# Beside work held to its tick on VectorE and ScalarE, GLA outputs one block later, value blocks in turning banks, matvec at 1.0 in the key stage

## The chip, the cores and the metric

The kernel runs on one core of a Trainium2 chip. Its engines work side by side, each through its own queue: TensorE (PE) multiplies matrices into the eight banks of PSUM, VectorE (DVE) and ScalarE (ACT) work element by element, GpSimd (POOL) and SyncE (SP) mostly issue transfers. The metric is the time of one execution in device microseconds, as the median of the runs shown. A second number, the span, is taken by the hardware profiler in one execution, from the first to the last instruction.

## The reference

One layer of a flow-matching backbone over 256 latent tokens with 256 context tokens, width 2048, all in f32. Cut to what matters here:

```python
qa, ka, va, qb, kb, vb, rb, lrf, lrb, gate_a, gate_b = jnp.split(h @ w_in, offs, axis=-1)
# A: 16 query and 4 key heads of 128, QK-norm, rotary, window of 128, context keys, sink
o_attn = windowed_attention(q, k, v, k_ctx, v_ctx, sink)
# B: gated linear attention, 4 heads (dk 256, dv 512), both directions, started from the context
of, _ = gla_chunked(q, k, v, gf, sf)
ob, _ = gla_chunked(flip(q), flip(k), flip(v), flip(gb), sb)
y_att = o_attn @ w_attn_o
y_gla = (rms_norm(o_gla, gla_norm).reshape(B, T, GLA_V_WIDTH) * jax.nn.silu(rb)) @ w_gla_o
x = x + mod_x[2] * ((jax.nn.sigmoid(gate_a) * y_att + jax.nn.sigmoid(gate_b) * y_gla) @ w_out)
x = x + mod_x[5] * conv_ffn(modulate(x, g_ffn, mod_x[3], mod_x[4]), w_up, conv_w, conv_b, w_down)
```

`mod_x` are six vectors of 2048, `silu(c) @ w_mod + b_mod`. Four of them (numbers 2 to 5) are made beside the main work: they are the matvec of this document.

## The kernel before

**Products.** Every f32 factor is split into two fp32r halves, hi and lo, and a product is three matmuls: hi·hi, lo·hi and hi·lo. Weights are streamed: `wload` (L180) brings two 128-row tiles by 512 columns, 512 KB, into one of seven buffers `raw`; `wsplit` (L186) makes `whi` on ScalarE and `wlo` on VectorE, with high priority for the scheduler. `proj_nat` (L195) multiplies one 512-column block of a weight matrix, step by step over two row tiles: first the hi products of all token blocks, then the lo products. Its accumulators are one PSUM bank for each token block (four for latent and context, two for the latent tokens alone), held over the whole block and emptied by `evac` at its end.

**PSUM.** Eight banks: four take turns under the tag `acc`; three, `side`, and one, `main`, serve the beside work (L61).

**Order.** `tick()` (L152) is called at the start of each step of a block. It sets `pin` to the last product issued, lowers the counters of the deferred pieces in `later` and calls those that are due (`defer(n, fn)` runs at the tick after n more), advances the generator in `beside` by its rate, and lets `pace()` take `bg_rate` steps of `bg_steps`. So the program says where beside work belongs. In the opening stage `in_order` ties each engine to that order. After it the framework's scheduler decides, when the kernel is built: it puts into each engine's queue what it expects to be ready, in the order of the program where there is a choice. What `mm_b` and `turn_b` (L82, L85) issue in a tick gets an edge (`after`, L75) that keeps it behind `pin`; the edge is of the class NoSync, so it fixes the order of building and is no semaphore. VectorE's and ScalarE's beside work has no such edge. Loads on SP have no order after the opening (L698).

**Stages around the change**, with what runs beside them:

| products | steps | beside |
|---|---|---|
| second half of the GLA keys, `kb_block` (L922) | 8 | GLA head 0 |
| GLA values of heads 1, 2, 3, `v_block` (L887) | 3 x 8 | GLA heads 1, 2, 3 |
| attention keys (L989), attention values (L990) | 2 x 8 | key norm and rotary, transposes `ptk` |
| four query blocks and the first gate block (L1064 to L1072) | 5 x 8 | attention of one key head each |
| GLA gate `rb` (L1101), merge (L1111 to L1135) | 4 x 8, 120 | transposes |
| `w_out` (L1177), ConvFFN | | matvec of `w_up`'s shift, then the last of `mod_x` |

The matvec (L316) runs through the first five rows: 96 steps for three vectors, each step one 512 KB `raw` load and two VectorE instructions (`macc`, L337 or L339); the load of the next step is issued with the step. Its rate is 0.3 a tick beside the GLA blocks, 1.6 in the key and value stage, 0.0 in the attention and 0.52 from the GLA gate on. After 8 steps a column block is transposed, summed (L345), and three ticks later `out` (L347) turns it by a small matmul into the bank `pcl`.

`gla_A` (L751) makes the two attention factors of a head in 13 pieces at 1.65 a tick: gates in two pieces, eight levels of which each takes exponentials (L812 to L820), products with q and k (L814, L821), running sums (L823 to L826) and, one piece later, matmuls into `pa`; then the scans and `kf`, `kg` (L844 to L853), and two pieces later the cross products with `kf` and `kg` (L860). `gla_o` (L866) multiplies both factors with the head's values, 24 matmuls into `po` for its two token blocks, and is called as soon as the value block is emptied, ahead of the next block. The values are split into hi and lo straight from their banks (`split`, L65).

The large SBUF tiles (`M`, L55) share 16 buffers.

Of the kernel before, what the change touches and what calls it, by code (L numbers as in the profile page):

```python
# [8 lines left out]
F32 = mybir.dt.float32  # L9
# [7 lines left out]
P = 128  # L17
# [8 lines left out]
QA, KA, VA, QB, KB, VB, RB = 0, 2048, 2560, 3072, 4096, 5120, 7168  # L26
# [4 lines left out]
MODB = [(t, 1) for t in range(4)] + [(t, 2) for t in range(4, 16, 2)]  # L31
DFF = 5632
SCALE = HD ** -0.5


def layer_kernel(ctx, tc, A, out):
    nc = tc.nc
    V, S, G, PE = nc.vector, nc.scalar, nc.gpsimd, nc.tensor
# [9 lines left out]
    acc = pool(name="acc", bufs=4, space=PSUM)  # L48
    ps = pool(name="ps", bufs=1, space=PSUM)

    w_in = A["w_in"][0]
# [6 lines left out]
    def W2(tag, name, shape, dt=F32):  # L58
        return f2.tile(shape, dt, name=name, tag=tag, bufs=F2_BUFS[tag])

    def bank(name, shape=(P, 512), side=False):  # L61

        return ps.tile(list(shape), F32, name=name, tag="side" if side else "main", bufs=3 if side else 1)

    def split(hi, lo, src):  # L65
        S.activation(hi, src, AF.Copy)  # L66
        V.tensor_tensor(lo, src, hi.bitcast(F32), op=ALU.subtract)  # L67
# [3 lines left out]
    def mm(*a, **k):  # L71

        last[0] = PE.matmul(*a, **k).ins  # L73

    def after(i):  # L75

        if pin[0] is not None:
            tc.add_manual_dep(i.ins, pin[0].name, mybir.DependencyInfo(
                mybir.DependencyClass.NoSync, mybir.DependencyReason.DATA), reason="place among the products")
        return i  # L80

    def mm_b(*a, **k):  # L82
        return after(PE.matmul(*a, **k))  # L83
# [54 lines left out]
    bg_rate = [0.0, 0.0]  # L138
# [5 lines left out]
    def defer(n, fn):  # L144

        later.append([n, fn])
# [5 lines left out]
    def tick():  # L152

        pin[0] = last[0]
        count[0] += 1
        for e in later:
            e[0] -= 1
        due = [e for e in later if e[0] < 0]
        later[:] = [e for e in later if e[0] >= 0]
        for e in due:  # L160
            e[1]()
        if beside:
            beside[2] += beside[1]
            while beside[2] >= 1.0:
                beside[2] -= 1.0
                next(beside[0], None)
        pace()
        pin[0] = None
# [26 lines left out]
    def proj_nat(w, r0, c0, kts, lhs, evac, get=wsplit, spare=0, banks=None):  # L195

        go = banks is None
        if go:
            banks = [bank("acx", side=True) if i < spare else acc.tile([P, 512], F32, name="acc", tag="acc")
                     for i in range(len(lhs))]  # L200
        for k0 in kts[::2]:
            tick()
            nk = min(2, kts[-1] + 1 - k0)
            hi, lo = get(w[r0 + k0 * P:r0 + (k0 + nk) * P, c0:c0 + 512])
            for i, l in enumerate(lhs):
                for k in range(nk):
                    kt = k0 + k
                    ahi, alo = l(kt)
                    mm(banks[i], ahi, hi[:, k, :], start=(go and kt == kts[0]), stop=False)
                    mm(banks[i], alo, hi[:, k, :], start=False, stop=False)  # L210
            if opening[0]:
                pace()
            for i, l in enumerate(lhs):
                for k in range(nk):
                    kt = k0 + k
                    mm(banks[i], l(kt)[0], lo[:, k, :], start=False, stop=(evac is not None and kt == kts[-1]))
        if evac is None:
            return banks
        for i in range(len(lhs)):
            evac(i, banks[i])  # L220
# [51 lines left out]
    ALL = list(range(KT))  # L272


    def mod_both(b):
# [37 lines left out]
        n_ = 16 // nk  # L313
        return [lambda i=i: get(i) for i in range(n_)], [lambda i=i: step(i) for i in range(n_)] + [fold]

    def matvec(parts, put=lambda fn: defer(3, fn)):  # L316


        seq = [(part, j, k0) for part in parts for j in range(part[4]) for k0 in range(0, KT, 2)]
        raws, a = {}, []  # L320

        def get(i):
            if i < len(seq) and i not in raws:
                (w, c0, _, _, _, _), j, k0 = seq[i]
                raws[i] = wload(w[k0 * P:k0 * P + 256, c0 + j * 512:c0 + (j + 1) * 512])

        def step(i):
            (_, _, vec, dst, _, b0), j, k0 = seq[i]
            get(i)
            get(i + 1)  # L330
            if k0 == 0:
                a[:] = [W2("mod", "macc", [P, 512])]
            raw = raws[i]
            for k in range(2):
                kt = k0 + k
                if kt == 0:
                    V.tensor_scalar(a[0], raw[:, 0, :], vec[:, 0:1], None, op0=ALU.mult)  # L337
                else:
                    V.scalar_tensor_tensor(a[0], raw[:, k, :], vec[:, kt:kt + 1], a[0],  # L339
                                           op0=ALU.mult, op1=ALU.add)  # L340
            if k0 == KT - 2:
                tr = W2("mod", "mtr", [P, 16, 32])
                V.transpose(tr.rearrange("p a c -> p (a c)"), a[0])
                rs = sm.tile([P, 16], F32, name="mrs", tag="mrs", bufs=2)
                V.tensor_reduce(rs, tr, op=ALU.add, axis=AX.X)  # L345

                def out():  # L347
                    pc = bank("pcl", (32, 16))
                    mm_b(pc, sel[:, 0:32], rs, start=True, stop=True)
                    pv = pc.rearrange("p (a b) -> p b a", b=4)  # L350
                    d = dst[:, 4 * j:4 * j + 4]
                    for b4 in range(4):
                        V.tensor_copy(d[32 * b4:32 * b4 + 32, :], pv[:, b4, :])
                    if b0 is not None:
                        V.tensor_tensor(d, d, bmod[:, b0 + j * 4:b0 + j * 4 + 4], op=ALU.add)

                put(out)

        return [lambda i=i: step(i) for i in range(len(seq))]
# [98 lines left out]
    h_xc = h_x + [h_tok(1, 0), h_tok(1, 1)]  # L458
# [61 lines left out]
    kbt = M("kb0", [P, 4, 512])  # L520
# [121 lines left out]
    for gi, (t0, n) in enumerate(groups):  # L642
# [28 lines left out]
        for b in run:  # L671
            keep = more and (b == "V" if gi % 2 == 0 else b[0] == "Q")
            banks = held.pop(b, None)
# [192 lines left out]
    def gla_o(h, a, vh, vl):  # L866
        ats, atc = a
        if h % 2 == 0:
            og.append(M(f"og{h}", [P, 2, 2, 512]))
        for t in range(2):  # L870
            po = bank("po", side=True)
            n = 0
            for s in range(4):
                if s < 2:
                    i = 0 if s == t else 1
                    ah, al = ats[i][:, 0, s, :], ats[i][:, 1, s, :]
                else:
                    ah = atc[0][:, s - 2, t * P:(t + 1) * P]
                    al = atc[1][:, s - 2, t * P:(t + 1) * P]
                for x_, y_ in ((ah, vh), (ah, vl), (al, vh)):  # L880
                    mm_b(po, x_, y_[:, s, :], start=(n == 0), stop=(n == 11))
                    n += 1
            S.activation(og[h // 2][:, h % 2, t, :], po, AF.Copy)
            junk = W2("fb", "junk", [P, 512])
            S.activation(junk, po, AF.Square, accum_out=ssg[:, h, t:t + 1])

    def v_block(c0, name):  # L887
        vh, vl = M(name + "h", [P, 4, 512], F32R), M(name + "l", [P, 4, 512], F32R)
        proj_nat(w_in, 0, c0, ALL, h_xc, lambda i, b: split(vh[:, i, :], vl[:, i, :], b))
        return vh, vl  # L890


# [20 lines left out]
    def with_gla(h, kb, block):  # L913
        res = []
        beside[:] = [gla_A(h, kb, qbt, res), 1.65, 0.0]
        v = block()
        for _ in beside[0]:
            pass
        beside.clear()
        return res, v  # L920
# [6 lines left out]
    a, kb1 = with_gla(0, kbt, kb_block)  # L927
    v = M("v0h", [P, 4, 512], F32R), M("v0l", [P, 4, 512], F32R)
    for i in range(4):
        split(v[0][:, i, :], v[1][:, i, :], vb0[:, i, :])  # L930
    gla_o(0, a, *v)
    for h in (1, 2, 3):
        a, v = with_gla(h, kb1 if h > 1 else kbt, lambda h=h: v_block(VB + h * 512, f"v{h}"))
        gla_o(h, a, *v)


    att = M("att", [P, 2048])
# [47 lines left out]

        defer(2 + i, turn)

    bg_rate[0] = 1.6
    proj_nat(w_in, 0, KA, ALL, h_xc, ka_evac)  # L989
    vah, val = v_block(VA, "va")  # L990

    oh, ol = [], []

# [17 lines left out]
    def attend(g, qT):  # L1011
# [3 lines left out]
        for t in range(2):  # L1015
# [14 lines left out]
            sk = sink[:, 4 * g:4 * g + 4]  # L1030
            V.scalar_tensor_tensor(mx, mx, SCALE, sk, op0=ALU.mult, op1=ALU.max)
            V.tensor_tensor(es, sk, mx, op=ALU.subtract)
            V.tensor_scalar(mx, mx, -1.0, None, op0=ALU.mult)
            S.activation(es, es, AF.Exp)
            for h in range(4):
                S.activation(sc[h], sc[h], AF.Exp, scale=SCALE, bias=mx[:, h:h + 1],  # L1036
                             accum_out=ds_[:, h:h + 1])
# [73 lines left out]
    for j in range(4):  # L1111
# [6 lines left out]
        def at_evac(t, b, a1=a1, j=j):  # L1118
            if j == 0:
# [5 lines left out]
                 lambda t, b, a2=a2: sig.append(S.activation(a2[t], b, AF.Sigmoid)))  # L1125
# [218 lines left out]
```

## Time and profile before

| | us |
|---|---|
| median of 3 runs | 2018.4 (2017.47 to 2019.22) |
| the profiled execution | 2015.55 |
| its span | 2013.3 |
| VectorE busy in it | 1447.0 |
| ScalarE busy in it | 970.6 |

A line of the view of waits names the instruction that waited and, after the arrow, what it waited for last; then the total time in us, how often, and the longest. A line of the timeline gives start and length in us, engine, line, operation, what is written and read, how many instructions are merged (x), and in brackets the idle time of the engine before them. A tile's name stands without its number. [...]

### The profile page before, as it was taken

The numbers are of one execution on the slowest core, as the hardware profiler recorded it, in microseconds if no ns is written. First come the engines' busy times: TensorE is split into PE (matmuls) and PEld (weight loads), VectorE is DVE, ScalarE is ACT, GpSimd is POOL, SyncE is SP. The second block draws the span as 40 slices with busy tenths as digits, with TensorE's granted clock in tenths as the row PEclk, the third lists the DMA queues.
The fourth block names the chain that finished last, engine by engine and source line by source line (L and its number), as shares of the span: only waits on it lengthen the run. The fifth ranks groups of instructions, "written<-read, shape, count | busy, mean of one in ns | idle before, by whom it ended". The sixth has DMA issues, their size and how long they took to land.

```text
span 2013.3 us, 27564 instructions
## 1 busy us (share of the span) xinstructions
PE 1985.8 (99%) x10452; PEld 1649.7 (82%) x10452; DVE 1447.0 (72%) x2246; ACT 970.6 (48%) x1415; POOL 37.2 (2%) x56
## 2 busy tenths in 40 slices
PE   9999999999999999999999999999999999999998
PEld 7778888887777777887778888888888888888887
DVE  5656767887758888877776476899897455667754
ACT  5223565552345656444344445665555434555532
POOL 0001000001000000000000000000000000000000
PEclk9999999999999999999999999999999999999999
DMA  9876222346543456788887586588885655555563
GB/s 390 330 274 218 92 83 86 102 125 205 171 156 116 129 187 203 254 278 270 272 272 239 189 313 209 179 267 270 265 273 199 211 197 189 188 188 188 189 215 110
DMA packets 200437, 417.41 MB, mean 207 GB/s; under 512 B 13040, under 2 KB 13456, under 8 KB 195696
## 3 DMA queue, kind: packets, MB, share of 16 engines
q1 hardware_dynamic: 198816, 411.48, 61.3%
q0 software_dynamic: 1056, 4.08, 0.6%
q8 instruction: 82, 1.34, 0.3%
q14 instruction: 51, 0.42, 0.1%
q10 hardware_dynamic: 432, 0.09, 0.0%
HBM read 413.48 MB, written 2.11 MB: 206 GB/s over the span
## 4 chain that ended last, share of the span: by engine, by line
PE 58%; DMA 5%; DVE 3%; issue 1%; ACT 0%; DVEq 0%; ACTq 0%
PE acc L73 43%; PE accs L73 12%; DMA raw<-in_w_mod 5%; DVE macc L339 2%; DVE wlo L67 1%; PE poa L83 1%; PE pS L83 1%; PE ptp L86 1%; PE pto L86 0%; ACT whi L66 0%; PE ptx L86 0%; DVE s L1041 0%; ACT s L1036 0%; DVE macc L337 0%; PE ptq L86 0%
## 5 line engine op out<-in xcount | busy, mean ns | idle before, releaser
L66 ACT ACTIVATE whi<-raw 128x1024 fp32r<-128x1024 f32 x536 | 567.5, 1059 | 701.3 <-PE acc L73 493.7
L67 DVE TENSOR_TENSOR wlo<-raw,whi 128x1024 fp32r<-128x1024 f32 x536 | 653.7, 1223 | 294.9 <-ACT whi L66 269.1
L339 DVE SCALAR_TENSOR_TENSOR macc<-raw,ccol,macc 128x512 f32<-128x512 f32 x240 | 181.0, 754 | 104.5 <-DMA raw<-in_w_mod 101.1
L73 PE MATMUL acc<-h,whi 128*128 128x512 f32 x672 | 183.8, 395 | 0.0
L73 PE MATMUL accs<-h,whi 128*128 128x512 f32 x672 | 180.3, 390 | 0.0
L73 PEld LDWEIGHTS accs<-h,whi 128*128 128x128 f32 x672 | 126.2, 188 | 28.2
L73 PE MATMUL acc<-whi,ah 128*128 128x512 f32 x352 | 137.1, 389 | 0.0
L73 PE MATMUL acc<-whi,al 128*128 128x512 f32 x352 | 137.1, 389 | 0.0
L73 PE MATMUL acc<-whi,h00hi 128*128 128x512 f32 x336 | 134.1, 399 | 0.5 <-DVE val L67 0.5
L73 PE MATMUL acc<-whi,h01hi 128*128 128x512 f32 x336 | 133.6, 398 | 0.0
L73 PE MATMUL acc<-whi,h00lo 128*128 128x512 f32 x336 | 131.9, 393 | 0.0
L73 PE MATMUL acc<-whi,h01lo 128*128 128x512 f32 x336 | 131.7, 392 | 0.0
L73 PEld LDWEIGHTS acc<-h,whi 128*128 128x128 f32 x672 | 115.6, 190 | 15.1
L73 PEld LDWEIGHTS acc<-h,wlo 128*128 128x128 f32 x672 | 102.7, 189 | 13.1
L73 PE MATMUL accs<-h,wlo 128*128 128x256 f32 x672 | 108.0, 283 | 0.0
L73 PE MATMUL acc<-h,wlo 128*128 128x256 f32 x672 | 106.8, 282 | 0.0
L73 PE MATMUL acc<-wlo,ah 128*128 128x512 f32 x352 | 94.1, 389 | 0.0
L73 PE MATMUL acc<-wlo,h01hi 128*128 128x512 f32 x336 | 93.0, 395 | 0.8 <-DVE wlo L67 0.7
L73 PE MATMUL acc<-wlo,h00hi 128*128 128x512 f32 x336 | 93.5, 393 | 0.1
L73 PEld LDWEIGHTS accs<-h,wlo 128*128 128x128 f32 x672 | 92.7, 192 | 0.0
L73 PEld LDWEIGHTS acc<-wlo,ah 128*128 128x128 f32 x352 | 66.1, 188 | 13.7
L73 PEld LDWEIGHTS acc<-whi,ah 128*128 128x128 f32 x352 | 66.1, 188 | 13.7
(406 smaller groups left out, 3668.0 us busy)
## 6 DMA issues: line engine op xcount, KB each, us to landing
raw<-in_w_in SPq DMA_DIRECT2D x204, 512.0 KB, 4.3
raw<-in_w_up SPq DMA_DIRECT2D x184, 512.0 KB, 3.5
raw<-in_w_mod SPq DMA_DIRECT2D x128, 512.0 KB, 4.2
raw<-in_w_down SPq DMA_DIRECT2D x88, 512.0 KB, 3.6
mraw<-in_k_wm SPq DMA_DIRECT2D x32, 1024.0 KB, 8.7
raw<-in_w_attn_o SPq DMA_DIRECT2D x32, 512.0 KB, 5.1
raw<-in_w_gla_o SPq DMA_DIRECT2D x32, 512.0 KB, 4.7
raw<-in_w_out SPq DMA_DIRECT2D x32, 512.0 KB, 4.7
```

The costliest lines, as they stand in the source:

```text
L66: S.activation(hi, src, AF.Copy)
L67: V.tensor_tensor(lo, src, hi.bitcast(F32), op=ALU.subtract)
L73: last[0] = PE.matmul(*a, **k).ins
L83: return after(PE.matmul(*a, **k))
L86: return after(PE.transpose(*a))
L339: V.scalar_tensor_tensor(a[0], raw[:, k, :], vec[:, kt:kt + 1], a[0], op0=ALU.mult, op1=ALU.add)
```

## The change

Four edits.

- `V` and `S` become wrappers that pass each instruction they issue through `after`. What VectorE and ScalarE get inside a tick is so kept behind the last product before that tick; outside ticks nothing changes, since `pin` is empty there.
- `gla_o` of each head is deferred by one tick count: it runs at the second tick of the next block instead of ahead of it.
- The value blocks of heads 1 and 3 take the bank `main` for their first accumulator (name `acm`), that of head 2 takes four `acc` banks, and the attention value block takes two `side` banks and two `acc` banks. Since `main` is then held by a block, the matvec's column sums `pcl` go to `side` until the key stage, and to `main` from there on.
- The matvec's rate in the key and value stage is 1.0 instead of 1.6.

```diff
+class Placed:
+    def __init__(self, engine, place):
+        self.engine, self.place = engine, place
+
+    def __getattr__(self, name):
+        f = getattr(self.engine, name)
+
+        def call(*a, **k):
+            return self.place(f(*a, **k))
+
+        return call
...
+    V = Placed(V, after)
+    S = Placed(S, after)
...
-            banks = [bank("acx", side=True) if i < spare else acc.tile([P, 512], F32, name="acc", tag="acc")
-                     for i in range(len(lhs))]
+            banks = [bank("acm") if spare < 0 and i == 0 else bank("acx", side=True) if i < spare else
+                     acc.tile([P, 512], F32, name="acc", tag="acc") for i in range(len(lhs))]
...
+    pcl_side = [True]
...
-                    pc = bank("pcl", (32, 16))
+                    pc = bank("pcl", (32, 16), side=pcl_side[0])
...
-    def v_block(c0, name):
+    def v_block(c0, name, spare=0):
...
-        proj_nat(w_in, 0, c0, ALL, h_xc, lambda i, b: split(vh[:, i, :], vl[:, i, :], b))
+        proj_nat(w_in, 0, c0, ALL, h_xc, lambda i, b: split(vh[:, i, :], vl[:, i, :], b), spare=spare)
...
-    gla_o(0, a, *v)
+    defer(1, lambda a=a, v=v: gla_o(0, a, *v))
     for h in (1, 2, 3):
-        a, v = with_gla(h, kb1 if h > 1 else kbt, lambda h=h: v_block(VB + h * 512, f"v{h}"))
-        gla_o(h, a, *v)
+        a, v = with_gla(h, kb1 if h > 1 else kbt, lambda h=h: v_block(VB + h * 512, f"v{h}", -(h % 2)))
+        defer(1, lambda h=h, a=a, v=v: gla_o(h, a, *v))
...
-    bg_rate[0] = 1.6
+    pcl_side[0] = False
+    bg_rate[0] = 1.0
     proj_nat(w_in, 0, KA, ALL, h_xc, ka_evac)
-    vah, val = v_block(VA, "va")
+    vah, val = v_block(VA, "va", 2)
```

## The prediction, made before the result was known

> **What bounds the kernel now.** I read the page's busy shares first, then its chain.
>
> ```profile
> PE 1985.8 (99%) x10452; PEld 1649.7 (82%) x10452; DVE 1447.0 (72%) x2246; ACT 970.6 (48%) x1415; POOL 37.2 (2%) x56
> ...
> PE 58%; DMA 5%; DVE 3%; issue 1%; ACT 0%; DVEq 0%; ACTq 0%
> ```
>
> TensorE is busy for 1985.8 of 2013.3 us, so the change, which removes no matmul, can win only what TensorE waits, and what it loses beside those waits. The chain still holds 5% DMA and 3% VectorE, so some waits reach the end. The next view is the waits of TensorE alone, from 214 us (the end of the opening) to 1240 us (past the last work that the change moves); columns: total us, times, longest.
>
> ```profile
> PE acc L73 <- DVE wlo L67: 4.7, 7, 1.6
> PE pa L83 <- DVE q L814: 3.0, 4, 0.9
> PE pa L83 <- DVE kf L852: 2.5, 4, 1.0
> PE po L83 <- DVE v3l L67: 2.5, 1, 2.5
> PE ptk L86 <- DVE sq L972: 1.9, 1, 1.9
> PE poa L83 <- DVE ptl L67: 1.1, 2, 0.9
> PE acc L73 <- DVE val L67: 0.5, 1, 0.5
> PE ptq L86 <- DVE sq L972: 0.4, 1, 0.4
> PE ptp L86 <- DVE s L1041: 0.4, 1, 0.4
> ```
>
> They add up to 17.0 us, and every one ends on VectorE. That sum is about all there is to win. So the question is what stands in VectorE's queue ahead of the awaited instruction. The timeline of VectorE at the end of the last value block answers it for v3l:
>
> ```profile
> 460.33 3.41 DVE L339 SCALAR_TENSOR_TENSOR macc<-raw,ccol,macc 128x512 f32<-128x512 f32 x4
> 463.67 0.68 DVE L67 TENSOR_TENSOR atc<-pa,atc 128x512 fp32r<-128x512 f32 x1
> 464.27 2.49 DVE L339 SCALAR_TENSOR_TENSOR macc<-raw,ccol,macc 128x512 f32<-128x512 f32 x3
> 466.67 1.48 DVE L67 TENSOR_TENSOR wlo<-raw,whi 128x1024 fp32r<-128x1024 f32 x1
> 468.07 2.47 DVE L67 TENSOR_TENSOR v3l<-acc,v3h 128x512 fp32r<-128x512 f32 x4
> ```
>
> Seven matvec instructions (macc, 3.41 + 2.49 = 5.9 us) run as a burst ahead of the four v3l splits, although the program spreads them over the ticks. The other form of the same fault shows at 930 us (VectorE, then TensorE) and at 521 us (VectorE):
>
> ```profile
> 930.74 1.54 DVE L339 SCALAR_TENSOR_TENSOR macc<-raw,ccol,macc 128x512 f32<-128x512 f32 x2 [2.85 <-DMA raw<-in_w_mod]
> 932.20 1.22 DVE L67 TENSOR_TENSOR wlo<-raw,whi 128x1024 fp32r<-128x1024 f32 x1
> ```
>
> ```profile
> 933.47 1.20 PE L73 MATMUL acc<-wlo,oh 128*128 128x512 f32 x4 [1.56 <-DVE wlo L67]
> ```
>
> ```profile
> 521.10 1.54 DVE L339 SCALAR_TENSOR_TENSOR macc<-raw,ccol,macc 128x512 f32<-128x512 f32 x2 [2.37 <-DMA raw<-in_w_mod]
> ```
>
> VectorE stands idle 2.85 us for a matvec load, the wlo that TensorE needs is queued behind it, and TensorE waits 1.56 us. The waits of VectorE from 475 to 1068 us, and the matvec instructions by stretch (stretch, its length, VectorE busy (count), clock, DMA share, GB/s), say how general this is:
>
> ```profile
> DVE macc L339 <- DMA raw<-in_w_mod: 80.9, 45, 3.6
> ```
>
> ```profile
> 568.00:798.00 230.00, 20.35 (x28) 1.00 0.51 160
> 798.00:1068.00 270.00, 72.30 (x99) 1.00 0.81 267
> 1068.00:1165.00 97.00, 1.23 (x2) 1.00 0.63 208
> ```
>
> Between 568 and 798 us the program asks for no matvec step (its rate is 0.0 there), yet 28 such instructions run: they were pulled forward to the moment at which their load was expected, and so they meet loads that are late.
>
> **The change part by part.** The kernel's order in each queue is set when it is built; the new edge holds VectorE's and ScalarE's beside work behind the last product before its tick.
>
> *Matvec held to its place, merge stages (910 to 1068 us).* A held step finds its load, issued a step earlier, landed. The 4.7 us of wlo waits should go; bounds 0 and 5.1 us, the idle of TensorE in the second of these rows (length first, then TensorE's busy time; clock and DMA share come ahead of the last number):
>
> ```profile
> 800.00:910.00 110.00, 109.99 (x499) 90.10 (x498) 87.02 (x113) 49.59 (x53) 0.00 (x0) 1.00 0.81 264
> 910.00:1068.00 158.00, 152.88 (x668) 121.22 (x667) 117.38 (x152) 61.68 (x64) 0.00 (x0) 1.00 0.81 269
> ```
>
> I take 4.0. The steps do not vanish. The program's rates give floor(32 x 0.3 + 16 x 1.6) = 35 of 96 steps by the end of the key stage before, and 25 after; the 28 early instructions go back too. So 71 steps are left for the 0.52 stage: 137 of its 152 ticks, 12 products each. A product costs 62.60 / 276 = 0.227 us by the chain's row
>
> ```profile
> 1105.79 62.60 PE acc L73 x276
> ```
>
> so 137 ticks last about 373 us, from 798 to some 1171 us: the 1068:1165 stretch, now empty of matvec, carries it at the rate of the stretch ahead of it. Its cover is VectorE's slack and the DMA share, 0.63 now and about 0.81 then. I take 0; if loads held up wlo there too, 5.1 / 158 x 103 = 3.3 us.
>
> *Attention (568 to 798 us).* The 28 instructions leave. I take 1.0 of the 1.1 us (poa) and leave the 0.4s; bounds 0 and 1.9.
>
> *Key stage at 1.0.* The transposes ptk wait 1.9 us for a VectorE chain in which the 2.37 us load wait at 521 us stands. At one step a tick instead of 1.6 VectorE also has 0.6 x 1.54 = 0.9 us less a tick. I take 1.5, bounds 0 and 1.9. The smaller val wait of 0.5 goes, because the attention value block now fills two side banks first, so that the query block's two banks are long free: 0.5, bounds 0 and 0.5.
>
> *GLA output in the next block.* For head 3 the 2.5 us wait goes: its 24 products come two ticks later, when v3l is done. With it goes a slow stretch just behind (start, us, then stretches with TensorE's clock third from the end):
>
> ```profile
> 469.88 0.63 PE L83 MATMUL po<-v3h,ats 128*128 128x512 f32 x1
> ...
> 473.25 0.63 PE L83 MATMUL po<-v3h,ats 128*128 128x512 f32 x2
> ```
>
> ```profile
> 469.00:473.30 4.30, 4.30 (x13) 3.39 (x13) 4.19 (x7) 0.19 (x1) 0.57 (x3) 0.60 0.69 239
> 530.50:533.00 2.50, 0.56 (x5) 0.40 (x5) 2.50 (x6) 0.00 (x0) 0.00 (x0) 1.00 0.45 168
> ```
>
> Eight products take 473.25 - 469.88 = 3.37 us where 8 x 0.227 = 1.82 would do: 1.5 us, while the granted clock was 0.60. The 1.94 us wait at 530 us left it at 1.00. Together 4.0, bounds 0 and 4.1. [...]
>
> *What the output covered.* Behind v1 and v2 those 24 products run while the banks are emptied. Where v1 ends, TensorE's first output product and VectorE's splits of banks two to four are
>
> ```profile
> 337.26 0.70 PE L83 MATMUL po<-v1h,ats 128*128 128x512 f32 x2
> ```
>
> ```profile
> 337.82 1.21 DVE L67 TENSOR_TENSOR wlo<-raw,whi 128x1024 fp32r<-128x1024 f32 x1
> 338.95 1.88 DVE L67 TENSOR_TENSOR v1l<-acc,v1h 128x512 fp32r<-128x512 f32 x3
> ```
>
> Afterwards the next block's products come there, at 337.26. The turning banks give it one free bank, four products, 0.9 us, until about 338.2; the second bank is free at 338.95 + 0.63 = 339.6: a wait of 1.4 us. Three boundaries (v1/v2, v2/v3, v3/keys) make 0 to 4.2 us. The nearest row is the val wait, 0.5 us, also an uncovered split; I take 0.55 each, 1.7 lost.
>
> *GLA chain held to its ticks.* Level 7 of head 2 runs ahead of its tick, whose products begin at 386.15; the last factor kf follows (VectorE, then TensorE):
>
> ```profile
> 382.81 0.69 DVE L814 TENSOR_TENSOR q<-q,qb 128x512 f32<-128x512 f32 x1 [0.18 <-ACT q L813]
> ...
> 393.69 0.69 DVE L852 TENSOR_TENSOR kf<-kf,kb 128x512 f32<-128x512 f32 x1
> ```
>
> ```profile
> 386.15 0.48 PE L73 MATMUL acc<-whi,h01hi 128*128 128x512 f32 x1
> ```
>
> The edge moves level 7 by 386.15 - 382.81 = 3.3 us, and by one wlo (1.22 us above) more if the tick's own split goes first: 4.5 us, and kf with it. The cover is the eighth step of the block, 24 x 0.227 = 5.4 us, which can run before the cross products, and the output no longer needs them at once. I take 0 for the chain; the bounds are a gain of the q and kf waits (5.5) and a loss of 4 x 4.5 = 18.0.
>
> *The rest.* The small column sums go to side banks, two products each, and nothing waits for them now: 0. The value tiles of a head live two ticks longer; 16 large tiles exist, and I count 16 in use at most: 0. The opening has its own fixed order: 0.
>
> Sum: -4.0 - 1.0 - 1.5 - 0.5 - 4.0 + 1.7 = -9.3 us. On the profiled span of 2013.3 that gives 2004.0, on that execution's 2015.55 it gives 2006.2. It lies 2.9 below the median of the runs, 2018.4; on the median the forecast is **2009.1 us**.
>
> **The rivals.**
>
> *Loads, not order, are the limit.* The held steps still meet late loads, since the DMA share of 0.81 lasts 103 us longer; the merge waits stay and 3.3 us come on top. For it: 45 late loads in the row above. Against: 800 to 910 us has the same share, 0.81, and TensorE idles 0.01 us there. Sum: -9.3 + 4.0 + 3.3 = -2.0, 2016.4 us.
>
> *The edges change little.* The builder's order stays nearly what it was, because most beside work already hangs on products that are held. Then only head 3, val and the boundaries count: -4.0 - 0.5 + 1.7 = -2.8, 2015.6 us. Against: matvec hangs on no product, and it makes the bursts.
>
> *The chain comes late (slower).* Level 7 and all behind it start 4.5 us later in each of four heads, and TensorE, which already waits for kf, waits for the whole delay: +18.0 - 9.3 = +8.7, 2027.1 us. From 9.3 / 4 = 2.3 us a head it eats the gain. For it: kf has no slack today. Against: 5.4 us of products to put in between.
>
> **How the numbers follow.** A measurement of this kernel can tell about 0.2%, 4.0 us, from no change. Forecast 0.62 (own range 2003 to 2014.6: from every gain at its bound, 13.5, with no boundary cost and a third of the GLA waits, to the merge and the key gain both gone); loads 0.17; little change 0.08; late chain 0.13. Faster takes nearly all of the forecast and the lucky part of the two middle cases, 0.67; same 0.20; slower, mainly the late chain, 0.13. The range runs from all 17.0 us of waits gone to the loads case with its boundaries at their worst (-2.0 + 2.5 = +0.5): 2001 to 2019.
>
> **What would show it.** Right: no macc wait on DMA of note, no matvec between 568 and 798 us, matvec until about 1175; po of head 3 inside the key block without the 0.60 clock; ptk and val waits near 0. Wrong: TensorE waiting at block starts for a value split for more than 4 us in all, for kf or q for more than 5.5 us, or wlo waits that reappear after 1068 us.

## The result and the profile after

| | before | after |
|---|---|---|
| median, us | 2017.93 (4 runs, 2015.1 to 2019.22) | 1995.16 (4 runs, 1994.34 to 1995.58) |
| ratio | | 0.9889, 95% interval 0.9871 to 0.9906 |
| span of the profiled execution, us | 2013.3 | 1993.2 |

The change is faster by 22.8 us between the medians and by 20.1 us between the spans; 9.3 were forecast, and 1995.2 lies below the range that was given (2001 to 2019). The direction was right, the size was not.

Where the time went is best read by stage. The views of the two kernels give, for three stretches that begin and end with the same product, the length, TensorE's busy time (instructions), then the weight loads, VectorE, ScalarE and GpSimd, the clock, the DMA share and GB/s. The stretches are: end of the opening to the first query block; query blocks, attention and GLA gate; merge. Before:

```profile
210.20:568.40 358.20, 347.55 (x1843) 292.94 (x1839) 263.40 (x484) 172.90 (x334) 28.70 (x35) 1.00 0.38 121
568.40:840.00 271.60, 269.43 (x1247) 213.14 (x1248) 227.27 (x429) 151.66 (x249) 0.57 (x1) 1.00 0.55 174
840.00:1182.00 342.00, 336.87 (x1487) 272.55 (x1486) 231.93 (x280) 142.74 (x148) 1.05 (x2) 1.00 0.76 254
```

After:

```profile
210.20:558.70 348.50, 344.40 (x1840) 292.02 (x1837) 248.01 (x460) 172.05 (x333) 23.70 (x35) 1.00 0.36 111
558.70:828.80 270.10, 269.12 (x1248) 212.91 (x1246) 223.13 (x420) 153.94 (x252) 0.57 (x1) 1.00 0.53 168
828.80:1161.90 333.10, 333.10 (x1488) 273.86 (x1487) 250.10 (x315) 142.75 (x148) 1.05 (x2) 1.00 0.83 285
```

So the first stretch gives 9.7 us, the second 1.5, the merge 8.9. The opening and all behind the merge are as they were. In the merge TensorE shows no idle time now, although VectorE has 18 us more to do there and the DMA share is higher. The waits of TensorE from 214 to 1240 us, 17.0 us before, are now

```profile
PE pa L101 <- DVE kf L46: 2.8, 4, 0.9
PE pa L101 <- DVE q L46: 1.1, 2, 0.7
PE ptq L104 <- DVE sq L46: 0.3, 1, 0.3
PE pcl L101 <- DVE mrs L46: 0.3, 1, 0.3
```

(all of VectorE's and ScalarE's instructions carry the wrapper's line, L46). The waits for wlo, v3l, ptk, poa and val are gone. The page says the same of VectorE's matvec steps: 1.5 us of idle time ahead of 240 instructions, where it was 104.5 (101.1 of it on loads).

```profile
L46 DVE SCALAR_TENSOR_TENSOR macc<-raw,ccol,macc 128x512 f32<-128x512 f32 x240 | 180.5, 752 | 1.5
```

```profile
PE 93%; DVE 3%; ACT 2%; DMA 1%; issue 1%; POOL 0%; DVEq 0%; ACTq 0%
```

The chain of work that ended last holds 93% TensorE and 1% DMA, where it was 58% and 5%.

### The profile page after: what moved, and what is told of

It reads as the page before. It is cut to its first block, busy times and chain, and to the rows that moved or that the text cites. A ratio compares the mean times of both kernels' runs of the same rounds, so it can differ in the third digit from the quotient of the medians.

```text
span 1993.2 us, 27537 instructions
## 1 busy us (share of the span) xinstructions
PE 1979.4 (99%) x10452; PEld 1651.1 (83%) x10452; DVE 1444.8 (72%) x2246; ACT 972.3 (49%) x1417; POOL 32.2 (2%) x56
## 4 chain that ended last, share of the span: by engine, by line
PE 93%; DVE 3%; ACT 2%; DMA 1%; issue 1%; POOL 0%; DVEq 0%; ACTq 0%
PE acc L88 66%; PE accs L88 12%; PE acx L88 3%; PE pa L101 2%; PE pm L312 2%; PE poa L101 1%; PE pS L101 1%; PE po L101 1%; PE ptp L104 1%; PE acm L88 1%; DVE wlo L46 1%; DMA raw<-in_w_in 1%; ACT ge L46 1%; ACT whi L46 1%; PE pss L442 0%
## 5 line engine op out<-in xcount | busy, mean ns | idle before, releaser
L46 ACT ACTIVATE whi<-raw 128x1024 fp32r<-128x1024 f32 x568 | 601.6, 1059 | 752.9 <-PE acc L88 478.5
L46 DVE TENSOR_TENSOR wlo<-raw,whi 128x1024 fp32r<-128x1024 f32 x568 | 694.9, 1225 | 372.3 <-ACT whi L46 318.1
L46 DVE SCALAR_TENSOR_TENSOR macc<-raw,ccol,macc 128x512 f32<-128x512 f32 x240 | 180.5, 752 | 1.5
L88 PE MATMUL acc<-whi,h01hi 128*128 128x512 f32 x304 | 121.1, 398 | 0.0
L88 PE MATMUL acc<-whi,h00hi 128*128 128x512 f32 x304 | 120.6, 397 | 0.0
L88 PE MATMUL acc<-whi,h01lo 128*128 128x512 f32 x304 | 119.4, 393 | 0.0
L88 PE MATMUL acc<-whi,h00lo 128*128 128x512 f32 x304 | 119.2, 392 | 0.0
L88 PE MATMUL acc<-wlo,h01hi 128*128 128x512 f32 x304 | 85.3, 394 | 0.0
L88 PE MATMUL acc<-wlo,h00hi 128*128 128x512 f32 x304 | 84.9, 392 | 0.0
L46 DVE SCALAR_TENSOR_TENSOR u<-us,cols,u 128x255 f32<-128x255 f32 x176 | 77.6, 477 | 0.5
```

The costliest lines, as they stand in the source:

```text
L46: return self.place(f(*a, **k))
```

## The experiments

The edits were taken apart first, then put back one at a time. Stage times are read off the traces at the same products as above; each ratio is to runs of the kernel before on the same chip.

| kernel | median, us | ratio to before (interval) | span | opening to query blocks | attention | merge |
|---|---|---|---|---|---|---|
| before | 2017.93 | | 2013.3 | 358.2 | 271.6 | 342.1 |
| changed | 1995.16 | 0.9889 (0.9871 to 0.9906) | 1993.2 | 348.6 | 270.1 | 333.1 |
| edges alone | 2005.47 | 0.9946 (0.9932 to 0.9961) | 2002.6 | 357.5 | 270.9 | 332.7 |
| all but the edges | 2014.30 | 0.9992 (0.9979 to 1.0004) | 2012.9 | 351.3 | 270.4 | 348.0 |
| edges on the matvec alone | 2007.35 | 0.9961 (0.9947 to 0.9976) | 2004.9 | 359.5 | 271.2 | 332.7 |
| edges on the rest alone | 2012.03 | 0.9975 (0.9962 to 0.9988) | 2012.3 | 354.3 | 271.9 | 342.9 |
| changed, rate 1.6 | 2003.69 | 0.9929 (0.9913 to 0.9946) | 2001.8 | 353.8 | 272.9 | 332.7 |
| changed, output not deferred | 1998.57 | 0.9905 (0.9890 to 0.9920) | 1996.2 | 351.1 | 269.8 | 333.1 |
| changed, banks not turned | 1998.99 | 0.9907 (0.9893 to 0.9922) | 1997.3 | 351.9 | 269.8 | 333.1 |
| changed, matvec loads held | 2196.78 | one run | 2194.9 | 392.1 | 314.8 | 372.4 |
| before, rate 1.0 | 2018.58 | 1.0009 (1.0000 to 1.0018) | 2016.6 | 353.7 | 271.2 | 349.4 |
| changed, cross products later | 1991.24 | 0.9877 (0.9863 to 0.9892) | 1989.3 | 344.6 | 270.1 | 333.1 |
| changed, rate 0.6 | 1996.30 | 0.9901 (0.9885 to 0.9918) | 1994.2 | 348.0 | 270.9 | 333.5 |

Spans and stages come from one profiled execution each. The opening takes 210.1 to 212.0 us in these traces, whatever the edit, so a span alone is good to about 2 us. The stages are better where the matvec is held: the executions of such a kernel differ by 1.0 to 2.6 us. Where it isn't, they differ by 4.1 to 12.4 us (edges on the rest alone: 2005.1 to 2017.5), so a difference of a few us in a stage of one of those kernels is weak by itself.

### The edges, alone and left out

```diff
+    V = Placed(V, after)
+    S = Placed(S, after)
```

The class `Placed` comes with it; nothing else of the change does.

> The kernel before with one of the four edits alone: the edges on VectorE and ScalarE. Theory (order of the matvec in VectorE's queue): the merge stage, first attn_o product to first w_out product, falls from 342.1 us to 333, as in the changed kernel; the burst ahead of v3l goes, and most of the 2.5 us wait and the slow stretch with it; span 1998 to 2001. Rival (deferral, banks and the lower rate carry it, since they change what VectorE has to do): merge stage above 338 us, span 2005 or more.

The merge came out at 332.7 us, as the theory has it, and the whole at 2002.6, 1.6 us above its span. The other half of what was expected did not come: the first stretch gains only 0.7 us. TensorE's waits show why:

```profile
PE pa L101 <- DVE kf L46: 2.8, 4, 0.9
PE pa L101 <- DVE q L46: 2.4, 4, 0.8
PE acc L88 <- ACT whi L46: 2.0, 2, 1.4
PE acc L88 <- ACT y L46: 1.6, 1, 1.6
PE po L101 <- DVE v1l L46: 1.2, 1, 1.2
PE pto L104 <- DVE sr L46: 1.2, 1, 1.2
PE acc L88 <- DVE val L46: 0.9, 1, 0.9
PE ptq L104 <- DVE sq L46: 0.4, 1, 0.4
```

The waits for v3l and ptk are gone, but products now wait 1.6 us for a bank that the key norm (y) has to empty, 1.2 us for v1l at the end of a value block, and twice, 2.0 us together, for whi in the attention value block, beside the norm and rotary work. The edges take the burst away; the crowd at the block ends stays.

The reverse, the changed kernel without the edges:

```diff
-    V = Placed(V, after)
-    S = Placed(S, after)
```

> The changed kernel without the edges: deferral, banks and rate 1.0 stay. Theory (order): merge stage about 342 us as before, macc still waits for loads some 80 us in all between 475 and 1068 us; only head 3 and the attention value block gain; span 2005 to 2009. Rival (the other three edits carry it): merge stage about 333 us, span 1994 to 2000.

The theory's numbers for the merge were too kind: 348.0 us, 5.9 more than before, and the span of 2012.9 is above the 2005 to 2009 expected. The first stretch gains 6.9 us, and the merge gives it back. TensorE waits there for wlo and VectorE for matvec loads. From TensorE's list of waits (214 to 1240 us):

```profile
PE acc L88 <- DVE wlo L82: 8.3, 8, 2.6
PE pa L99 <- DVE kf L870: 3.4, 4, 1.2
```

And from VectorE's (214 to 1260 us):

```profile
DVE macc L357 <- DMA raw<-in_w_mod: 94.9, 59, 4.2
```

Against 4.7 and 87.6 us in the same windows before, the fault has grown: the lower rate of the key stage sends more steps into the merge (111 matvec instructions run there, 92 before), and unheld they meet late loads there. Two waits for wlo, of 2.6 and 2.4 us, also had a lower clock behind them: 0.61 from 1017 to 1021 us and 0.71 from 1084.5 to 1088.5 us.

### Whose edges

Only the matvec steps, called by `pace`, get the edges; then all other beside work does and the matvec doesn't.

```diff
+    in_pace = [False]
+    def held(i):
+        return after(i) if in_pace[0] else i
+    V = Placed(V, held)
+    S = Placed(S, held)
...
+        in_pace[0] = True
         bg_rate[1] += bg_rate[0]
         while bg_rate[1] >= 1.0 and bg_steps:
             bg_rate[1] -= 1.0
             bg_steps.pop(0)()
+        in_pace[0] = False
```

> The kernel before with edges on the matvec steps alone. Theory (the matvec's place is the cause): the same as with all edges within 2 us, merge stage 333 us, no macc wait on loads, span 1998 to 2002. Rival (the edges on the GLA and attention chains do it): span above 2008, merge stage 340 or more.

> The kernel before with edges on all beside work except the matvec steps. Theory (the matvec's place is the cause): within 3 us of before, span 2010 to 2015, merge stage about 342 us. Rival (GLA and attention chains): span below 2005. A late GLA chain, the rival on the slower side of the prediction, would show here as more than 5.5 us of waits for q and kf.

The matvec's edges alone give the whole of the merge (332.7 us, no wait of macc on a load); the span of 2004.9 is 3 us above the expected range, because the first stretch, 359.5 us, gains nothing without the rest. The others' edges alone leave the merge at 342.9 and win 3.9 us in the first stretch. Waits for q and kf are 3.0 and 3.2 us. That is 6.2, above the 5.5 us named as the sign of a late GLA chain, but 5.5 was the sum before: the chain costs 0.7 us more at most, where the prediction's slower rival had 18.

### The other three edits, taken back one at a time

```diff
-    bg_rate[0] = 1.0
+    bg_rate[0] = 1.6
```

> The changed kernel with the key stage's matvec rate back at 1.6. Theory (the late loads and the burst were the fault, not the number of steps): with held steps VectorE has room, ptk waits at most 1 us, merge stage 333 us as it is, span 1993 to 1995. Rival (VectorE is too full in the key stage at 1.6): ptk waits 1.5 to 2.5 us again and the span is 1995 to 1998.

The rival's wait comes, 2.4 us for ptk, and the span of 2001.8 lies above both ranges, 8.6 us over the changed kernel. The timeline of TensorE at the first key transposes, and the clock of the stretch behind it (third from the end):

```profile
527.18 0.63 PE L104 MATMUL ptk<-ident,sq 128*128 128x128 f32 x4 [2.40 <-issue]
...
529.43 0.63 PE L88 MATMUL acx<-whi,h00hi 128*128 128x512 f32 x1
529.86 0.63 PE L88 MATMUL acx<-whi,h00lo 128*128 128x512 f32 x1
```

```profile
528.00:532.00 4.00, 4.00 (x13) 3.12 (x12) 4.00 (x8) 0.45 (x1) 0.00 (x0) 0.58 0.33 87
```

ptk comes 2.40 us late (its row names no releaser), and then the products follow each other at 0.43 us from start to start instead of 0.23, while the granted clock is 0.58 over the 4 us. TensorE waits a second time, 2.0 us, for the GLA gate's transposes (pto, 794 us). The attention stage, which holds that wait, takes 272.9 us, 2.0 more than at rate 0.6, where the wait for pto is 1.8 us; by an estimate, a second such stretch of 3.4 us would account for 1.7 of them. With it, two waits and 1.7 us lost behind each make 2.4 + 2.0 + 3.4 = 7.8 of the 8.6 us. The pair at pto, 3.7 of them, isn't shown to come from the number of steps: the wait of 1.8 us appears at rate 0.6 too, further down, and none at 1.0.

```diff
-    defer(1, lambda a=a, v=v: gla_o(0, a, *v))
+    gla_o(0, a, *v)
...
-        defer(1, lambda h=h, a=a, v=v: gla_o(h, a, *v))
+        gla_o(h, a, *v)
```

> The changed kernel with the GLA output back ahead of the next block; edges, banks and rate 1.0 stay. Theory A (the outputs are what waited: they stand right behind a value split that VectorE and ScalarE bring late): TensorE waits for v1l, v2l or v3l again for 2 to 5 us in all, and the stages from the opening's end to the query blocks take 352 to 355 us instead of 348.6. Theory B, that of the prediction (the output covers the emptying of the banks, and its leaving costs 1.7 us): 347 to 348 us.

Neither theory: the stage takes 351.1 us, 2.5 more, but no product waits for a value split. What waits is q, the start of the next head's chain:

```profile
PE pa L101 <- DVE q L46: 3.2, 4, 1.4
PE pa L101 <- DVE kf L46: 2.8, 4, 0.9
```

3.2 us as against 1.1 with the output deferred. The output's copies and squares (ScalarE, L883 and L885 of the kernel before) stand between a head's gates and the block end; that they are what delays q was not tried by itself.

```diff
-        a, v = with_gla(h, kb1 if h > 1 else kbt, lambda h=h: v_block(VB + h * 512, f"v{h}", -(h % 2)))
+        a, v = with_gla(h, kb1 if h > 1 else kbt, lambda h=h: v_block(VB + h * 512, f"v{h}"))
...
-    vah, val = v_block(VA, "va", 2)
+    vah, val = v_block(VA, "va")
```

> The changed kernel with all value blocks on the four acc banks; edges, deferral and rate 1.0 stay. Theory A (the turning banks are why the uncovered boundaries cost nothing): TensorE waits at four boundaries for a bank being emptied, 0.5 to 2 us each, 2 to 8 us in all, span 1995 to 2001. Theory B (the boundaries cost nothing in any case, since the emptying is fast enough): within 1 us of the changed kernel, 1992 to 1994.

Theory A by its span (1997.3), though only two of the four boundaries wait, 1.5 us for v1l and 0.5 for val:

```profile
PE acc L88 <- DVE v1l L46: 1.5, 1, 1.5
PE pa L101 <- DVE q L46: 1.1, 2, 0.7
PE acc L88 <- DVE val L46: 0.5, 1, 0.5
```

The rest of the 3.3 us by which the first stretch grows isn't in the list of waits. The span grows by 4.1, of which 1.0 lies in the opening, ahead of the edit, so 3.3 us is the better price of the banks.

```diff
-    bg_rate[0] = 1.6
+    bg_rate[0] = 1.0
```

This is the kernel before with that line alone.

> The kernel before with the matvec rate of the key stage at 1.0 and nothing else. Theory (the rate helps the key stage, and only pays where the steps that it sends on are held): the stages from the opening's end to the query blocks gain 1 to 4 us, the merge stage grows by 2 to 7 us over 342.1, as in the kernel with all but the edges (348.0); span 2010 to 2017. Rival (the rate pays by itself): merge stage about 342, span below 2010.

The first stretch gains 4.5 us, the merge loses 7.3, and the whole is the same within 0.2%. With the kernel that has all but the edges, where the merge loses 5.9, and the two held kernels, where it is 332.7 at 1.6 and 333.1 at 1.0, this says that the rate pays only where the steps that it sends on are held.

### Two more looks

```diff
-    def wload(src):
+    def wload(src, held=False):
...
-        load(raw[:, 0:n, :], src.rearrange("(c p) d -> p c d", p=P))
+        d = load(raw[:, 0:n, :], src.rearrange("(c p) d -> p c d", p=P))
+        if held and pin[0] is not None:
+            tc.add_manual_dep(d, pin[0].name, mybir.DependencyInfo(
+                mybir.DependencyClass.NoSync, mybir.DependencyReason.DATA), reason="place among the products")
...
-                raws[i] = wload(w[k0 * P:k0 * P + 256, c0 + j * 512:c0 + (j + 1) * 512])
+                raws[i] = wload(w[k0 * P:k0 * P + 256, c0 + j * 512:c0 + (j + 1) * 512], True)
...
             get(i)
-            get(i + 1)
```

> The changed kernel with each matvec load held to the tick of its own step instead of being issued a step ahead. Theory (a matvec step in VectorE's queue whose load is late starves wlo, and the edge helps because the load is then long done): macc waits for loads again, more than 20 us in all, and the merge stage grows by 3 us or more over 333.1. Rival (the edge helps by spacing the steps, whatever their loads do): merge stage within 1 us of 333.1, whether or not macc waits.

A miss: 2194.9 us, and yet macc never waits for a load. The list of SP's waits shows another loop:

```profile
SPq L124 <- DVE wlo L46: 834.9, 468, 14.0
SPq L124 <- DVE macc L46: 587.8, 145, 30.4
```

SP waits 587.8 us (119.4 in the changed kernel) for buffers that held matvec steps give back, and the weight loads stand behind in the same queue. The run doesn't tell the two theories apart; whether a late load or the bare position of a step is what hurts rests on the trace of the kernel before, read below.

```diff
         yield
         yield
+        yield
+        yield
         pa = bank("pa", (P, 2, T), side=True)
```

> The changed kernel with the cross products of each GLA head moved from its eighth tick to just behind the block. Theory (kf is late at that tick and nothing else wants the cross products before the next block's second tick): the 2.8 us of waits for kf go, span 1989 to 1991.5. Rival (the wait moves: the factor atc or the banks come late at the block's end): span 1993 to 1998, with waits on kf, v or atc in place of the old ones.

The four waits for kf are gone, none of their size takes their place (pcl, 0.3 before, is 0.9), and the span falls by 3.9 us to 1989.3:

```profile
PE pa L101 <- DVE q L46: 1.1, 2, 0.7
PE pcl L101 <- DVE mrs L46: 0.9, 1, 0.9
PE ptq L104 <- DVE sq L46: 0.3, 1, 0.3
```

Its runs, 1991.1 to 1993.5 us, all lie below those of the changed kernel (1994.3 to 1995.6). The intervals of the two ratios overlap, so against the changed kernel the gain rests on the trace; against the kernel before it is clear.

```diff
-    bg_rate[0] = 1.0
+    bg_rate[0] = 0.6
```

> The changed kernel with the key stage's rate at 0.6. Theory (at 1.0 VectorE already meets the norm and rotary work in time): within 1 us, span 1992 to 1994. Rival (VectorE is still the bound there): span 1990 to 1992, by hidden stretches of the products in the key stage.

The first stretch is 348.0 us, within 1 us as the theory says; the span of 1994.2 is just above its range, with a 1.8 us wait for pto in the attention stage that the changed kernel doesn't have. VectorE is not the bound of the key stage at 1.0.

## Why the prediction was wrong in its size

The mechanism was right: the matvec, pulled forward to the moment at which its load was expected, held up wlo, and the edges on it alone take the merge from 342.1 to 332.7 us. The step that failed is the one that took TensorE's listed idle time for about all there is to win: 17.0 us in all, which set the low end of the range, and 5.1 in the merge. The change won 22.8 us between the medians, 20.1 between the spans and 8.9 in the merge, because the starts of products were later than the idle time shows. Some smaller terms were mis-sized too, and one reading of the trace was false.

**The merge, 4.0 forecast, 8.9 measured.** The upper bound of 5.1 us was itself too small. It was TensorE's idle time, and that leaves out part of every wait. Two products of the kernel before, neighbours on TensorE:

```profile
944.26 0.39 PE L73 MATMUL acc<-whi,ol 128*128 128x512 f32 x1
945.52 0.50 PE L73 MATMUL acc<-wlo,oh 128*128 128x512 f32 x1 [0.87 <-DVE wlo L67]
```

The second starts 1.26 us after the first, where 0.227 is usual: it is 1.03 us late, and the row says 0.87, since a product's bar lasts 0.39 us, 0.16 longer than its turn. Shorter delays don't appear at all: the late products of the merge whose rows list no idle time are up to 0.12 us late. The lists hold a hint that was not used in the sum, the waits of the weight loads from 840 to 1182 us before, of which none on wlo is left after:

```profile
PEld acc L73 <- DVE wlo L67: 11.1, 15, 2.0
```

Counted by starts, 49 products of the merge came over 0.03 us late before, 10.7 us together, and 22 after, 2.1 us together: 8.6 of the 8.9 us. The better bound was at hand: 120 steps of 12 products and 32 transposes of 0.11 us need 1440 x 0.227 + 3.5 = 330 us, 12 less than before.

The same count tells what the products waited for. Of the 49, 29 are products of wlo, two at most to each of fifteen `wlo` instructions, and they hold 8.8 of the 10.7 us. Each of the fifteen stands one to three places behind a matvec instruction that had waited for its load, as at 945.52:

```profile
942.79 1.54 DVE L339 SCALAR_TENSOR_TENSOR macc<-raw,ccol,macc 128x512 f32<-128x512 f32 x2 [3.24 <-DMA raw<-in_w_mod]
944.25 2.35 DVE L67 TENSOR_TENSOR wlo<-raw,whi 128x1024 fp32r<-128x1024 f32 x2
```

In every case that load wait (0.6 to 3.6 us) is longer than the delay of the product. In the changed kernel no late product is one of wlo, and no matvec instruction waits for a load. So the late load is what hurt; that spacing alone would have helped as much is not shown by any run.

**Held steps in the longer matvec stretch, 0 forecast, 0 measured**, although the DMA share rose to 0.83; the rival of the loads is refuted. The reading beside it was false, though: of 28 matvec instructions between 568 and 798 us only six were early. The products of the GLA gate, where the rate of 0.52 begins, start at 726 us while the last key head's attention still runs, and 22 of the instructions lie behind that:

```profile
568.00:720.00 152.00, 3.74 (x5) 1.00 0.46 141
720.00:726.00 6.00, 0.74 (x1) 1.00 0.39 116
726.00:798.00 72.00, 15.87 (x22) 1.00 0.64 204
```

The same holds for the forecast of where held steps end: from 716 to 828 us the changed kernel runs 34 matvec instructions, and the last before `w_out` ends at 1117 us, not at about 1175. The attention stage gained 1.5 us all the same; 1.0 was forecast.

**What the output covered, 1.7 lost by forecast, 0 measured.** The working gave the free bank four products, 0.9 us. In the changed kernel TensorE's order at that boundary is another:

```profile
335.67 0.61 PE L101 MATMUL pz<-wgl 128*128 128x512 f32 x2
336.12 0.39 PE L88 MATMUL acc<-whi,h00hi 128*128 128x512 f32 x1
...
339.52 0.39 PE L88 MATMUL acc<-whi,h00lo 128*128 128x512 f32 x1
339.75 0.39 PE L88 MATMUL acc<-whi,h10hi 128*128 128x512 f32 x1
```

The builder lets the first token block run ahead on the free bank through two steps and the hi products of the third: 16 products, 339.75 - 336.12 = 3.6 us, and the banks behind it are emptied by then. Without the turning banks the same boundary waits 1.5 us, the size that was worked out (1.4).

**The GLA chain, 0 forecast.** Its waits for q fell from 3.0 to 1.1 us, while those for kf rose by 0.3 only. In head 2, VectorE's level 7 starts 394.53 - 382.81 = 11.7 us ahead of the cross products before and 392.98 - 383.62 = 9.4 us after; kf is waited for 0.64 us in both. So the edges take 2.3 us of the lead, less than the 3.3 to 4.5 that the working gave, and it costs nothing. The run without deferral puts the gain for q down to the deferred output (3.2 against 1.1). The first stretch, 4.3 forecast, gave 9.7: its listed waits fell from 10.4 to 3.9 us, 1.5 came with the full clock, and the remaining 1.7 us are in no list; delays that lists leave out, as in the merge, are likely, but not shown.

**Key stage at 1.0, 1.5 forecast.** From the kernel before it was the right size (ptk waited 1.9). What was missed is how the edits hang together: with all the other edits but at 1.6 the stage has a ptk wait of 2.4 us and a half-clock stretch behind it. With the edges alone, also at 1.6, no ptk wait is listed; the waits for whi and y, 3.6 us, stand there instead. By the ratios the edges alone give 0.54%, the other three edits alone 0.08%, not clear of nothing, and all four together 1.11%. In the merge that is plain: without the edges the lower rate costs 5.9 us there, with them 0.4.

**Head 3's output, 4.0 forecast**: the wait for v3l and the half-clock stretch are both gone; the clock of the changed kernel is 1.00 in the three stretches given with the result. The edges alone remove this wait, and so do the other three edits alone. The slower rival, the late chain, and the rival in which the edges change little are refuted: kf and q wait 3.9 us in the changed kernel, 5.5 before, and the edges on the matvec alone give the whole of the merge.

## What to carry to other kernels

Where a compute engine is busy for 99% of the span, bound a gain by counting its instructions at their usual spacing, not by the idle time that the profile lists: in the merge the list held 5.1 of the 10.7 us that the starts show. Background work that streams its own operands belongs behind the foreground in the engine's queue, at a place where its load has long landed (the merge took 332.7 us with the matvec held so, 342.1 without); moved work pays or costs by that place, so test a rate and an order together. A spare accumulator at a block boundary is worth more than its own few products if the order can run ahead on it: 3.6 us of products here, where its own four make 0.9.

## What the runs showed of the hardware

In the kernel before, TensorE's granted clock (third from the end) stood at 0.50 for 3.41 us behind the wait of 2.52 us for v3l. The stretch of the same length ahead of that holds 0.97 us of TensorE's work, the first number after the length:

```profile
466.36:469.77 3.41, 0.97 (x4) 0.84 (x5) 3.41 (x5) 0.60 (x2) 3.21 (x6) 1.00 0.81 248
469.77:473.18 3.41, 3.41 (x9) 2.67 (x9) 3.30 (x6) 0.07 (x1) 0.00 (x0) 0.50 0.61 225
```

Over 4 us behind a wait the clock was 0.61 and 0.71 with all but the edges (waits of 2.6 and 2.4 us for wlo), 0.57 with the edges on the matvec alone (2.12 us for v3h, 0.64 for v3l right behind it) and 0.58 at rate 1.6 (2.40 us for ptk). A stretch of 3.41 us at half clock costs 1.7 us, an estimate from its length and its clock; eight products in the one above took 3.37 us instead of 1.82. No other wait of the kernel before, up to 1.94 us, has such a stretch behind it: its clock is 1.00 from 5.56 to 469.76 us and from 473.19 to 2012.50 us. Length alone doesn't tell, though. The kernel before at rate 1.0 waits 2.37 us for v3l and keeps its clock:

```profile
468.60 0.50 PE L83 MATMUL po<-v3l,ats 128*128 128x512 f32 x1 [2.37 <-DVE v3l L67]
```

```profile
468.00:474.00 6.00, 5.40 (x24) 4.46 (x25) 4.97 (x7) 1.17 (x3) 0.40 (x2) 1.00 0.61 178
```

In the traces of the kernel before and the changed one the clock changes at times that lie whole multiples of 3.4133 us apart: full clock for 464.21 us (136 of them), half for 3.41 and full for 1539.41 (451) before, full for 1979.73 (580) after. Cut at these marks, from 5.56 us on before and 10.58 after, the stretch just ahead of a drop holds 0.97 us of TensorE's work as above, and at the two ends, where the products have run out, 0.00 before and 1.01 after; no other stretch of the two holds less than this one, of the kernel before:

```profile
930.57:933.98 3.41, 1.85 (x8) 1.23 (x8) 3.20 (x4) 1.18 (x3) 0.00 (x0) 1.00 0.52 165
```

So in these two traces a drop stands behind 0.00 to 1.01 us of work between two marks, and none behind 1.85 or more. Where the marks lie in the execution at rate 1.0, no view here shows. By an estimate, a mark in the middle of its wait would leave 3.41 - 2.37 / 2 = 2.2 us of work in the stretch on either side, more than the 1.85. What the runs do show is that of two waits for v3l, the one of 2.52 us cost 1.5 us more behind it, by the eight products, and the one of 2.37 us left the clock at 1.00.
